# Two modulation products: row scaling on ScalarE and summing by accumulating DMAs, in place of fused multiply-adds on VectorE

## The chip, the cores and the metric

The kernel runs on one core of one Trainium2 chip. The metric is the time of one execution on the device in microseconds (us). Beside it stands one execution that the hardware profiler recorded, with every instruction of TensorE (PE, and PEld for its weight loads), VectorE (DVE), ScalarE (ACT), GpSimd (POOL) and SyncE (SP), and every DMA.

## The reference, cut to what matters

The program is a chain of four layers with 512 tokens of width 2048. The change touches only the modulation vectors of layers 3 and 4. They depend on one vector c and not on the tokens:

```python
def ada_modulation(c, w_mod, b_mod):
    m = jax.nn.silu(c) @ w_mod + b_mod
    shift, scale, gate = jnp.split(m, 3, axis=-1)
    return shift[:, None, :], scale[:, None, :], gate[:, None, :]
...
h = rms_norm(x, norm_g) * (1.0 + scale) + shift
out = mixer(h)
x = x + gate * out
```

There are two such products (`ab` and `sg`), each of a vector of 2048 with a matrix of 2048 x 6144.

## The kernel before

All large products run on PE as three matmuls each (`mm3`, L167: high by high, high by low, low by high), with weights that stream from HBM. SP loads a chunk of 128x1024 (`w_load`, L135), ACT rounds it to its high part (`w_high`, L150), DVE subtracts to get the low part (`w_low`, L156). The order of every engine's instructions is the order in which the program text issues them. SP has the weight loads and the loads of the modulation matrices; POOL has the loads and stores of the residual stream (L590, L483) and the small DMAs.

The main products call `pump()` (L86) after every 12 matmuls or so. A pump resumes each side task once (evictions, attention heads, gates) and then resumes the first background task `bg_rate` times. The two modulation products are that background task. `bg_rate` is 1 in layers 1 (from the second product on, for 32 pumps), 2 and 3; it is 2 in items j = 1 and j = 2 of the first out projection (`out_proj` with i = 0, L586, 16 pumps each), and 0 elsewhere in the out projections and in the rest of layer 1.

`modulation` (L1283) goes through the parts scale, shift, gate, and in each through four column blocks of 512. For one block it loads 16 tiles of 128x512 (256 KB each, L1293), two ahead of their use, and adds them up in `acc` on DVE: the first by `tensor_scalar` (L1299), the other 15 by `scalar_tensor_tensor` (L1301), with the column `sc[:, k]` of silu(c) as scalar. Each resume does one tile. Then it waits `bg_rate` resumes, splits `acc` into a high and a low part (`split`, L173: ACT rounds at L174, DVE subtracts at L175), waits again, lets PE add over the partitions with a matrix of ones (L1310, L1311), waits again, and copies the row of sums (L1315) to DRAM (L1316, from POOL). When a part is done, POOL loads it as columns (L1318) and DVE adds the bias (L1322).

The tiles `acc`, `raw`, `hi`, `lo` and `row` come from the pool `s` of 28 buffers, which nearly all side work uses too. PE executes its instructions in program order, those of the modulation among the matmuls of the item that is running.

Of the kernel before, what the change touches and what calls it, by code (L numbers as in the profile page):

```python
# [9 lines left out]
AF = mybir.ActivationFunctionType  # L10
ALU = mybir.AluOpType
# [4 lines left out]
D = 2048  # L16
KC = 16
# [3 lines left out]
LOOK = 1  # L21
# Between two layers, after each two k of: the last units' second token half, the next layer's first half, its second half.
# S sums of squares, P their 1/rms across partitions, c an operand chunk of this half, d one of the first half,
# h and l the two parts of a weight chunk. SCH_END: the same for the output.
SCH = [["", "", "S", "h", "Pl", "hc", "cl", "hc"],
       ["l", "h", "S", "", "Pl", "", "c", "c"],
       ["", "", "d", "hd", "dl", "d", "hd", "dl"]]
SCH_END = ["", "S", "", "P", "c", "c", "c", "c"]


class Core:
# [197 lines left out]
    def tm_item(self, evac, first=None, need=None, n=512):  # L229
        """first: the operand comes token half by token half, first.ensure(half, k) makes it."""  # L230
        ps = [self.ps() for _ in range(NT)]
        for half in range(2):
            if first and half == 0:
                cs = []
                for hf in range(2):
                    for c in range(4):
                        if hf == 0:
                            cs.append(self.w_get(1))
                        for kk in range(2):
                            k = 2 * c + kk  # L240
                            first.ensure(hf, k + LOOK)
                            for t in (2 * hf, 2 * hf + 1):
                                self.tm_mm(ps[t], t, *cs[c], kk, k, k == 0, False)
                            first.tick(1 + hf, k, c + kk if hf else 3 - c)
                            if kk:
                                self.pump()
                continue
            for c in range(4):
                if need and c == half == 0:
                    need(0)  # L250
                h, l = self.w_get(1 if need and half == 0 else LAG)
                for kk in range(2):
                    k = half * 8 + 2 * c + kk
                    if need:
                        need(k)
                    if first:
                        first.ensure(0, k + 2)
                        first.ensure(1, k + 2)
                    for t in range(NT):
                        self.tm_mm(ps[t], t, h, l, kk, k, k == 0, k == KC - 1, n)  # L260
                    if self.final_read:
                        self.final_read(k)
                    if k < KC - 1 and (kk or n == 512):
                        self.pump()
        self.add(evac(ps))
        self.pump()
# [21 lines left out]
    def fg_last(self, kperm, bd):  # L288
        """The last two units, token half by token half."""
        ps = [self.ps() for _ in range(2)]  # L290
        po = lambda hf, u: ps[hf][:, u * 256:(u + 1) * 256]
        cs = []
        for hf in range(2):
            sl = slice(256 * hf, 256 * hf + 256)
            for c in range(4):
                if hf == 0:
                    cs.append(self.w_get(4 - c))
                for kk in range(4):
                    i = 4 * c + kk
# [53 lines left out]

    # -- start: x from the input; 1/rms is applied to the first layer's products
    def start(self):
# [65 lines left out]

    # during a layer's last products: the mix that is done takes the place of operands that nothing reads any more
    def mix_early(self, kperm, mixk):
# [13 lines left out]

    # -- out projection of a layer, feature by feature: B gets x_new * gain, xd[i] the residual stream
    def out_proj(self, i, kperm, mixk, gain, gate=None, fg=None, shift=None, rx=None, final=False, dump=False):
# [187 lines left out]

    # ---------------- layer 1
    def plan1(self):
# [6 lines left out]
    def layer1(self):  # L636
        nc, a = self.nc, self.a
        P = dict(zip(("convw", "convb", "ba", "bx", "lam"), (0, 32, 40, 56, 72)))
# [22 lines left out]

        # log sigmoid of lambda, times 4, and half biases
        lsg = self.fix.tile([128, 32], F32, name="lsg")
# [309 lines left out]

    # ---------------- layer 2
    def plan2(self):
# [305 lines left out]

    # ---------------- modulation rows
    def modulation(self, w, i):  # L1283
        nc = self.nc
        for part in (1, 0, 2):
            for j in range(4):
                c0 = part * D + j * 512
                acc = self.s()
                raws = []
                for k in range(KC + 2):  # L1290
                    if k < KC:
                        raw = self.s()
                        nc.sync.dma_start(out=raw, in_=w[k * 128:(k + 1) * 128, c0:c0 + 512])  # L1293
                        raws.append(raw)
                    if k >= 2:
                        raw = raws.pop(0)
                        ck = self.sc[:, k - 2:k - 1]
                        if k == 2:
                            nc.vector.tensor_scalar(out=acc, in0=raw, scalar1=ck, scalar2=None, op0=ALU.mult)  # L1299
                        else:  # L1300
                            nc.vector.scalar_tensor_tensor(out=acc, in0=raw, scalar=ck, in1=acc, op0=ALU.mult, op1=ALU.add)  # L1301
                        yield
                for _ in range(self.bg_rate):
                    yield
                hi, lo = self.sr(), self.sr()
                self.split(hi, lo, acc)
                for _ in range(self.bg_rate):
                    yield
                ps = self.ps()
                nc.tensor.matmul(out=ps, lhsT=self.ones, rhs=hi, start=True, stop=False)  # L1310
                nc.tensor.matmul(out=ps, lhsT=self.ones, rhs=lo, start=False, stop=True)  # L1311
                for _ in range(self.bg_rate):
                    yield
                row = self.s()
                nc.scalar.copy(out=row[0:1], in_=ps[0:1])  # L1315
                nc.gpsimd.dma_start(out=self.md[i][part:part + 1, j * 512:(j + 1) * 512], in_=row[0:1])  # L1316
            dst = self.mcol[:, i, part]
# [21 lines left out]

    # ---------------- layer 3  # L1340
    def plan3(self):
# [148 lines left out]

    # ---------------- layer 4
    def plan4(self):
# [111 lines left out]

    # ---------------- whole
    def run(self):
# [41 lines left out]

# [1 line left out]

# [30 lines left out]
def layout(inp):  # L1681
    d = {}
# [3 lines left out]
    w = inp["even_w_in"][0]  # L1686
# [14 lines left out]
    c, s = np.cos(ang).astype(f), np.sin(ang).astype(f)  # L1701
# [15 lines left out]
    d["lruw"] = np.stack([wa[0], wa[1], wx[0], wx[1]], 2).reshape(8, 128, 512)  # L1717
    # layer 2
    w = inp["odd_w_in"][0]
# [12 lines left out]
    for nm in ("ab", "sg"):  # L1732
        d[nm + "_wm"] = inp[nm + "_w_mod_2"][0]
    # layer 3
    w = inp["ab_w_in_2"][0]
# [14 lines left out]
    d["bias3"] = np.where(cnt > 0, np.log(np.maximum(cnt, 1)) * 128.0 ** 0.5, -1e30).astype(f)  # L1750
    # layer 4
    w = inp["sg_w_in_2"][0]
# [30 lines left out]
```

## Time and profile before

| | before |
|---|---|
| median of 3 runs (us) | 3378.86 |
| lowest and highest (us) | 3377.93, 3380.07 |
| span of the profiled execution (us) | 3376.1 |
| busy, PE and PEld | 99%, 82% |
| busy, DVE | 56% |
| busy, ACT | 36% |
| busy, POOL | 3% |

The span counts from the first to the last instruction of the profiled execution. Busy time on PE is modelled and overlaps: a matmul of 512 columns stands as 0.39 us, and the next one starts about 0.23 us after it. So PE's pace is read from the starts, and its idle time from the waits. Instructions that only issue a DMA count as no busy time.

### The profile page before, as it was taken

To read this page: it belongs to the slowest core of one execution; us is meant where nothing else is said; L and a number is where in the kernel's file an instruction comes from. 1 tells how busy PE (TensorE), PEld (TensorE's weight loads), DVE (VectorE), ACT (ScalarE), POOL (GpSimd) and SP (SyncE) were. 2 spreads that over 40 slices of the span, in tenths; PEclk is the share of its full clock that TensorE was granted. 3 is DMA by queue.
4 is the path that set the end of the run, shared out by engine and by line. 5 is a ranking of instruction groups with operands and counts; after the bars stand their busy time and mean duration, and the time that the engine had idled before them with its cause. 6 is when DMAs were issued, how large, how long until landed. Compare 5 with 4: busy or idle time off the path is not lost.

```text
span 3376.1 us, 40334 instructions
## 1 busy us (share of the span) xinstructions
PE 3354.3 (99%) x15596; PEld 2766.4 (82%) x15596; DVE 1894.8 (56%) x3179; ACT 1223.4 (36%) x1966; POOL 113.5 (3%) x208
## 2 busy tenths in 40 slices
PE   9999999999999999999999999999999999999998
PEld 7888888888888888888888888888888888888887
DVE  7766676568656566564576665544434526533334
ACT  5355553343333233344542322322333424222332
POOL 0000000100000000001000000000000000000000
PEclk9999999999999999999999999999999999999999
DMA  5422235645454445444344444322333422223232
GB/s 207 153 81 81 76 103 182 202 133 173 153 162 152 157 153 179 136 156 145 123 141 156 149 161 171 109 88 88 112 125 129 144 96 88 97 97 107 95 107 92
DMA packets 155088, 443.92 MB, mean 131 GB/s; under 512 B 19429, under 2 KB 19557, under 8 KB 154896
## 3 DMA queue, kind: packets, MB, share of 16 engines
q1 hardware_dynamic: 140832, 398.95, 35.5%
q0 software_dynamic: 14064, 42.40, 4.0%
q8 instruction: 122, 2.00, 0.2%
q14 instruction: 70, 0.57, 0.1%
HBM read 424.36 MB, written 16.91 MB: 131 GB/s over the span
## 4 chain that ended last, share of the span: by engine, by line
PE 99%; DVE 0%; DMA 0%; ACT 0%; issue 0%; SPq 0%; DVEq 0%; ACTq 0%
PE ps L169 32%; PE ps L171 32%; PE ps L170 32%; PE ps L178 2%; DMA raw<-in_w1t 0%; PE ps L1310 0%; PE ps L1311 0%; PE ps L519 0%; DVE s L529 0%; PE ps L505 0%; DVE l L156 0%; SPq L366 0%; ACT h L150 0%; ACT B L484 0%; ACT s L479 0%
## 5 line engine op out<-in xcount | busy, mean ns | idle before, releaser
L169 PE MATMUL ps<-Ah,h 128*128 128x512 f32 (+1 forms) x3200 | 1240.2, 388 | 0.0
L171 PE MATMUL ps<-Ah,l 128*128 128x512 f32 (+1 forms) x3200 | 1230.1, 384 | 0.0
L170 PE MATMUL ps<-Al,h 128*128 128x512 f32 (+1 forms) x3200 | 1225.2, 383 | 0.0
L156 DVE TENSOR_TENSOR l<-raw,h 128x1024 fp32r<-128x1024 f32 (+2 forms) x559 | 675.0, 1209 | 735.4 <-ACT h L150 726.5
L150 ACT CAST h<-raw 128x1024 fp32r<-128x1024 f32 (+2 forms) x559 | 577.3, 1035 | 863.2 <-PE ps L170 503.0
L171 PEld LDWEIGHTS ps<-Ah,l 128*128 128x128 f32 x3200 | 601.7, 188 | 127.9
L170 PEld LDWEIGHTS ps<-Al,h 128*128 128x128 f32 x3200 | 602.1, 188 | 122.8 <-issue 0.2
L169 PEld LDWEIGHTS ps<-Ah,h 128*128 128x128 f32 x3200 | 602.3, 188 | 117.4 <-issue 0.2
L169 PE MATMUL ps<-h,Ah 128*128 128x512 f32 (+2 forms) x1408 | 547.9, 389 | 7.1 <-ACT h L174 5.8
L170 PE MATMUL ps<-l,Ah 128*128 128x512 f32 (+2 forms) x1408 | 543.9, 386 | 0.8 <-DVE l L156 0.8
L171 PE MATMUL ps<-h,Al 128*128 128x512 f32 (+2 forms) x1408 | 544.2, 386 | 0.4
L169 PEld LDWEIGHTS ps<-h,Ah 128*128 128x128 f32 x1408 | 265.5, 189 | 64.1 <-ACT h L174 5.8
L171 PEld LDWEIGHTS ps<-h,Al 128*128 128x128 f32 x1408 | 265.2, 188 | 60.9 <-DVE Al L551 1.6
L170 PEld LDWEIGHTS ps<-l,Ah 128*128 128x128 f32 x1408 | 265.4, 189 | 57.9 <-DVE l L156 1.1
L1301 DVE SCALAR_TENSOR_TENSOR s<-s,sc 128x512 f32<-128x512 f32 x360 | 268.8, 747 | 5.8 <-DMA s<-in_ab_wm 1.7
L175 DVE TENSOR_TENSOR s<-ps,s 128x512 fp32r<-128x512 f32 (+2 forms) x178 | 101.1, 569 | 153.8 <-ACT s L174 153.7
L174 ACT CAST s<-ps 128x512 fp32r<-128x512 f32 (+2 forms) x178 | 86.1, 491 | 242.9 <-PE ps L178 168.1
L169 PE MATMUL ps<-s 128*128 128x512 f32 (+2 forms) x384 | 131.6, 343 | 0.0
L171 PE MATMUL ps<-s 128*128 128x512 f32 (+2 forms) x384 | 129.5, 337 | 1.3 <-DVE s L175 1.3
L170 PE MATMUL ps<-s 128*128 128x512 f32 (+2 forms) x384 | 128.8, 335 | 0.0
L476 ACT ACTIVATE s<-s 128x512 f32<-128x512 f32 (+1 forms) x72 | 42.0, 583 | 136.3 <-DVE s L468 73.3
L171 PEld LDWEIGHTS ps<-s 128*128 128x128 f32 x384 | 72.5, 189 | 10.2 <-DVE s L175 1.5
(271 smaller groups left out, 2026.6 us busy)
## 6 DMA issues: line engine op xcount, KB each, us to landing
raw<-in_wo SPq DMA_DIRECT2D x128, 512.0 KB, 3.5
raw<-in_w3f SPq DMA_DIRECT2D x112, 512.0 KB, 3.5
s<-in_ab_wm SPq DMA_DIRECT2D x192, 256.0 KB, 4.2
s<-in_sg_wm SPq DMA_DIRECT2D x192, 256.0 KB, 4.1
raw<-in_w2t SPq DMA_DIRECT2D x88, 512.0 KB, 3.6
raw<-in_w4f SPq DMA_DIRECT2D x64, 512.0 KB, 3.5
raw<-in_w1f SPq DMA_DIRECT2D x48, 512.0 KB, 3.6
raw<-in_w2f SPq DMA_DIRECT2D x32, 512.0 KB, 3.6
```

What stands on the lines that cost most here:

```text
L150: self.nc.scalar.copy(out=h[:, 0:n], in_=raw[:, 0:n])
L156: self.nc.vector.tensor_tensor(out=l[:, 0:n], in0=raw[:, 0:n], in1=h[:, 0:n].bitcast(F32), op=ALU.subtract)
L169: mm(out=out, lhsT=lh, rhs=rh, start=start, stop=False)
L170: mm(out=out, lhsT=lh, rhs=rl, start=False, stop=False)
L171: mm(out=out, lhsT=ll, rhs=rh, start=False, stop=stop)
L174: self.nc.scalar.copy(out=h, in_=src)
L175: self.nc.vector.tensor_tensor(out=l, in0=src, in1=h.bitcast(F32), op=ALU.subtract)
L178: self.nc.tensor.transpose(out, src, self.idt)
L476: nc.scalar.activation(out=sq[0], in_=xn, func=AF.Square)
L1301: nc.vector.scalar_tensor_tensor(out=acc, in0=raw, scalar=ck, in1=acc, op0=ALU.mult, op1=ALU.add)
```

## The change

`modulation` now takes two column blocks at a time, each with its own `acc`, and goes through their 32 tiles in turn. The first tile of a block is loaded into `acc` itself. Each tile is loaded three resumes ahead, and ACT scales it in place (`activation`, Copy, `scale=sc[:, k]`). From the second tile of a block on, the scaled tile is put on a list, and one resume later POOL issues a DMA that adds it to `acc` (`accum_op=add`, SBUF to SBUF). No DVE instruction is left in this loop. After the last tile the remaining sum is issued, three resumes are waited, and then the two blocks are split, summed over the partitions and stored one after the other as before. The other lines of the diff drop comments.

```diff
         for part in (1, 0, 2):
-            for j in range(4):
...
-                    if k >= 2:
+            for jj in range(2):
+                acc = [self.s() for _ in range(2)]
+                col = lambda j: slice(part * D + (2 * jj + j) * 512, part * D + (2 * jj + j + 1) * 512)
+                raws, sums = [], []
+                for n in range(2 * KC + 3):
+                    if n < 2 * KC:
+                        k, j = divmod(n, 2)
+                        raw = acc[j] if k == 0 else self.s()
+                        nc.sync.dma_start(out=raw, in_=w[k * 128:(k + 1) * 128, col(j)])
                         raws.append(raw)
+                    if n >= 3:
+                        k, j = divmod(n - 3, 2)
                         raw = raws.pop(0)
-                        ck = self.sc[:, k - 2:k - 1]
-                        if k == 2:
-                            nc.vector.tensor_scalar(out=acc, in0=raw, scalar1=ck, scalar2=None, op0=ALU.mult)
-                        else:
-                            nc.vector.scalar_tensor_tensor(out=acc, in0=raw, scalar=ck, in1=acc, op0=ALU.mult, op1=ALU.add)
+                        nc.scalar.activation(out=raw, in_=raw, func=AF.Copy, scale=self.sc[:, k:k + 1])
+                        if k:
+                            sums.append((acc[j], raw))
+                    raw = None
+                    if len(sums) > (1 if n < 2 * KC + 2 else 0):
+                        x, y = sums.pop(0)
+                        nc.gpsimd.dma_start(out=x, in_=y, accum_op=ALU.add)
+                        x = y = None
+                    if n >= 3:
                         yield
+                while sums:
+                    x, y = sums.pop(0)
+                    nc.gpsimd.dma_start(out=x, in_=y, accum_op=ALU.add)
+                    x = y = None
+                for _ in range(3):
+                    yield
+                for j in range(2):
+                    hi, lo = self.sr(), self.sr()
+                    self.split(hi, lo, acc[j])
...
```

## Rows read from the trace of the kernel before

**Rows 1.** The page's head and part 1: busy us, share, instructions
```profile
span 3376.1 us, 40334 instructions
...
PE 3354.3 (99%) x15596; PEld 2766.4 (82%) x15596; DVE 1894.8 (56%) x3179; ACT 1223.4 (36%) x1966; POOL 113.5 (3%) x208
```

**Rows 2.** Waits of PE, us 690 to 1660: us in total, times, longest
```profile
PE ps L171 <- DVE s L175: 1.3, 1, 1.3
PE ps L178 <- DVE s L1170: 0.4, 1, 0.4
```

**Rows 3.** Busy time by stretch: us, engines busy (instructions), granted clock, DMA share, GB/s
```profile
0.00:14.00 14.00, 7.62 (x21) 5.19 (x22) 3.87 (x9) 5.41 (x8) 4.08 (x11) 1.00 0.80 269
...
18.00:22.00 4.00, 4.00 (x14) 3.15 (x13) 4.00 (x9) 3.39 (x6) 0.00 (x0) 0.66 1.03 394
...
544.00:633.00 89.00, 89.00 (x390) 73.00 (x389) 54.80 (x72) 29.35 (x38) 11.36 (x20) 1.00 0.75 255
...
820.00:832.00 12.00, 10.30 (x74) 9.34 (x73) 10.38 (x29) 5.29 (x13) 2.33 (x4) 1.00 0.68 210
...
1680.00:2146.00 466.00, 465.89 (x2053) 379.81 (x2054) 303.96 (x492) 146.35 (x231) 4.66 (x8) 1.00 0.46 154
...
3360.00:3377.00 17.00, 4.23 (x27) 3.25 (x25) 7.70 (x18) 1.72 (x5) 0.00 (x0) 0.67 0.50 190
```

**Rows 4.** Lines L1301, L1299: count, ns minimum/median/maximum, first and last start
```profile
L1301 DVE SCALAR_TENSOR_TENSOR s<-s,sc x360: 644/747/754, 61.8 to 2145.9; 128x512 f32<-128x512 f32 x180
...
L1299 DVE TENSOR_SCALAR s<-s,sc x24: 477/481/489, 59.4 to 2091.6; 128x512 f32<-128x512 f32 x24
```

**Rows 5.** ACT by line and shape: busy us, mean ns, idle before and releaser
```profile
L174 ACT CAST s<-s 128x512 fp32r<-128x512 f32 x58 | 35.0, 618 | 117.0 <-DVE s L1379 101.3 <-DVE s L1301 14.2 <-DVE s L834 1.5
...
L479 ACT ACTIVATE s<-s,cols 128x512 f32<-128x512 f32 x14 | 9.9, 709 | 0.0
```

**Rows 6.** Timeline of PE, first out projection: start, us, instruction (13th after the first)
```profile
566.22 0.39 PE L169 MATMUL ps<-Ah,h 128*128 128x512 f32 x1
...
568.97 0.39 PE L169 MATMUL ps<-Ah,h 128*128 128x512 f32 x1
```

**Rows 7.** Timeline of DVE, us 543 to 566
```profile
543.90 1.53 DVE L1301 SCALAR_TENSOR_TENSOR s<-s,sc 128x512 f32<-128x512 f32 x2
...
551.92 0.69 DVE L175 TENSOR_TENSOR s<-s 128x512 fp32r<-128x512 f32 x1 [0.43 <-ACT s L174]
...
557.12 1.54 DVE L1301 SCALAR_TENSOR_TENSOR s<-s,sc 128x512 f32<-128x512 f32 x2
...
559.71 1.53 DVE L1301 SCALAR_TENSOR_TENSOR s<-s,sc 128x512 f32<-128x512 f32 x2
```

**Rows 8.** Timeline of POOL: the loads at the start of item j = 2
```profile
588.90 1.13 POOL L590 DMA_DIRECT2D s<-in_x  x2
```

**Rows 9.** DMA issues, us 544 to 633: count, KB each, median us to landing
```profile
s<-in_ab_wm SPq DMA_DIRECT2D x41, 256.0 KB, 6.0
...
xd<-s POOLq DMA_DIRECT2D x8, 256.0 KB, 6.2
...
md<-s POOLq DMA_DIRECT2D x3, 2.0 KB, 4.9
```

**Rows 10.** Line L483 (POOL's stores from SBUF), us 1480 to 1660
```profile
L483 POOL DMA_DIRECT2D xd<-s x14: 540/542/545, 1539.0 to 1656.2; - x14
...
DMA to landing us min/median/max: 2.3/2.3/2.6
```

**Rows 11.** Waits of POOL, us 544 to 640
```profile
POOL mcol L1318 <- DMA md<-s: 4.7, 1, 4.7
```

**Rows 12.** DMA issues, us 832 to 1152: a POOL load in layer 2
```profile
s<-rd POOLq DMA_DIRECT2D x6, 256.0 KB, 6.0
```

**Rows 13.** Timeline of all engines, us 815 to 842
```profile
823.39 0.49 DVE L1299 TENSOR_SCALAR s<-s,sc 128x512 f32<-128x512 f32 x1 [1.18 <-DMA s<-in_ab_wm]
...
828.71 0.19 PEld L171 LDWEIGHTS ps<-s 128*128 128x128 f32 x1 [1.50 <-DVE s L175]
```

More of the change, by code (lines that the diff above doesn't have):

```diff
@@ L1285, in modulation @@
         for part in (1, 0, 2):
-            for j in range(4):
[L1287 to L1293, printed above, removed]
+            for jj in range(2):
[7 more added lines that the diff above has]
+                        nc.sync.dma_start(out=raw, in_=w[k * 128:(k + 1) * 128, col(j)])
@@ L1303, in modulation @@
-                for _ in range(self.bg_rate):
-                    yield
[L1305 to L1313, printed above, removed]
@@ L1314, in modulation @@
-                row = self.s()
-                nc.scalar.copy(out=row[0:1], in_=ps[0:1])
-                nc.gpsimd.dma_start(out=self.md[i][part:part + 1, j * 512:(j + 1) * 512], in_=row[0:1])
+                        nc.scalar.activation(out=raw, in_=raw, func=AF.Copy, scale=self.sc[:, k:k + 1])
[6 more added lines that the diff above has]
+                        x = y = None
@@ new lines, in modulation @@
+                    if n >= 3:
+                        yield
+                while sums:
[3 more added lines that the diff above has]
+                for _ in range(3):
+                    yield
+                for j in range(2):
+                    hi, lo = self.sr(), self.sr()
+                    self.split(hi, lo, acc[j])
+                    for _ in range(self.bg_rate):
+                        yield
+                    ps = self.ps()
+                    nc.tensor.matmul(out=ps, lhsT=self.ones, rhs=hi, start=True, stop=False)
+                    nc.tensor.matmul(out=ps, lhsT=self.ones, rhs=lo, start=False, stop=True)
+                    for _ in range(self.bg_rate):
+                        yield
+                    row = self.s()
+                    nc.scalar.copy(out=row[0:1], in_=ps[0:1])
+                    nc.gpsimd.dma_start(out=self.md[i][part:part + 1, (2 * jj + j) * 512:(2 * jj + j + 1) * 512], in_=row[0:1])
```

## The prediction

> **What bounds the kernel now.** I read the page's busy times first, then PE's waits, then the table by stretch, then the pace of PE in its timeline. PE is busy for 3354.3 of 3376.1 us [rows 1]; DVE, which the change relieves, for 56%. Of the 21.8 us in which PE is idle, most lie where no modulation runs: 6.4 us in the first 14 us and some 12 us after us 3360, up to the span's end [rows 3]. In between, PE waits for DVE twice, for 1.3 and 0.4 us [rows 2], both around 826 us in layer 2. So a free DVE can give back 1.7 us at the most. The pace of PE between waits is 12 matmuls in 568.97 - 566.22 = 2.75 us [rows 6]. The change adds and removes no matmul. What is left to ask is whether it makes PE wait.
>
> **The change part by part.** *Removed from DVE:* 360 x 0.747 + 24 x 0.481 = 280 us [rows 4]. It lies beside PE's work and gives the path at most the 1.7 us above.
>
> *Added to ACT:* 384 scalings. The nearest row is L479, the same Copy with a column as scale from SBUF to SBUF, at 0.709 us [rows 5]: 272 us, which takes ACT from 1223 to 1495 us, 44% of the span. In the fullest stage, us 544 to 633, 38 scalings add 27 us to 29 busy of 89 [rows 3]. PE hides that; without that cover it would be the 272 us.
>
> *A scaling waits for its tile's load.* DVE had this wait before. Queued behind it on ACT are now the weight roundings (L150) and the roundings that feed PE. The load is issued three resumes ahead instead of two, so in the steady state I cost it at nothing. In layer 2 at 823 us, where pumps follow each other without an item's matmuls, DVE waited 1.18 us for such a load and PE 1.50 us for DVE a little later [rows 13]. There the new order has the first scaling of a pair of blocks two pumps later (step 34 of layer 2, counted as below). The bounds are -1.7 us (PE's waits for DVE go) and +6.0 us (a whole landing [rows 9]); I take 0, since one wait replaces another of its kind.
>
> *Added to POOL:* 360 DMA issues at 0.54 us each, as a store of the same tile costs [rows 10], 194 us on an engine that is busy for 113. But POOL takes its instructions in order, and each accumulation must wait until the previous one on the same `acc` has landed; POOL's load of `md` shows such a wait on one of its own DMAs, 4.7 us [rows 11]. With two sums in turn, each `acc` gets one accumulation per two resumes, and a block is a chain of 15 landings. The Trainium skill (DMA: Bandwidth & Descriptors, Rules for kernel authors) states the same: two accumulations on the same bytes need a wait for the first one's semaphore. Without that order there would be no chain, and the sum would be 0.
>
> *At rate 1* a round of the chain has two pumps, 5.5 us at the pace of rows 6 and more with attention in between: in layer 3 some 110 tiles took 466 us, 8.5 us per round. A load on POOL's queue in layer 2 lands in 6.0 us [rows 12]. That fits, and the last accumulation has four pumps before the split. I cost it at nothing.
>
> *At rate 2*, in items j = 1 and 2 of the first out projection, both resumes fall in one pump: DVE's pairs at 557.12 and 559.71 us show it [rows 7]. Between the first pair (543.90 [rows 7]) and the loads of item j = 2 (588.90 [rows 8]) lie 16 pumps, so a pump is 2.8 us and a round must land in 2.8 us. I count the 64 resumes of this stage in the new code. The 32 of layer 1 have just done the first pair's tiles. Its end takes 3 + 2 x 4 = 11. The second pair takes steps 12 to 43 for the tiles; its first accumulation goes out at step 15 (pump 8, 543.9 + 7 x 2.8 = 563.5 us); the first split is at step 47, and the first matmul with ones at step 49, in pump 25. PE ended item j = 0 just before 543.3 us, so it gets there at 543.3 + 25 x 2.8 = 613.3 us. That matmul stands in PE's own order, so no prefetched weights help it: it waits for the 15th landing, ACT's rounding (0.62 us [rows 5]) and DVE's subtraction (0.69 us [rows 7]). With L for issue to landing, the stall is 563.5 + 15 L + 1.3 - 613.3 = 15 L - 48.5 us, which is zero up to L = 3.2 us.
>
> *What is L?* No accumulating DMA is in the trace. From below: POOL's store of the same 256 KB where the queues are quiet, 2.3 us [rows 10], which reads only once. From above: the same store in this very stage, 6.2 us; there the modulation loads take 6.0 and even a 2 KB store 4.9 [rows 9]. The DMA engines are 75% busy here at 255 GB/s [rows 3], which is 340 GB/s when busy, so 256 KB in one pass cost 0.77 us. The 34 accumulations of the stage add 26 us (one pass) or 52 us (two reads of SBUF) to 67 of 89 us: 104% to 134%. So the engines stay full while loads go on, and I take L = 6.1 us until PE stalls: 8 rounds, to 612.3 us. Once PE stands, the weight loads stop, and L falls to the quiet store plus a second pass, 2.3 + 0.77 = 3.07: 7 rounds take 21.5 us. The chain ends at 633.8, and the stall is 633.8 + 1.3 - 613.3 = 21.8 us. The bounds are 0 (L below 3.2) and 15 x 6.1 - 48.5 = 43 us.
>
> The Trainium skill (DMA: Bandwidth & Descriptors, Anatomy of one DMA) gives a fixed 2.0 us plus the bytes at 436 GB/s for a DMA of POOL, 2.6 us for 256 KB as an estimate. By that rule the chain would keep up and the sum would be 0; the quiet store agrees with it and the store in this stage does not.
>
> *A stall's price on the clock.* After its idle time at the start PE has a mean granted clock of 0.66 from 18 to 22 us [rows 3], a mix of 2.4 and 1.2 GHz, which loses 0.34 x 4 = 1.4 us. I add that once, with 0 and 2 x 1.4 as bounds.
>
> *The buffers.* Tiles that wait for the chain stay in the pool of 28. At pump 21 about 14 rounds are due and 7 done, so some 14 tiles more are held, and SP may stand at a modulation load with weight loads behind it. That starves PE by another door, but ends when the same chain ends; I add nothing.
>
> Sum against the profiled execution: 3376.1 + 21.8 + 1.4 = 3399.3 us; the median of the runs lies 2.8 us above that span, so 3402 us.
>
> **The rivals.** *The chain keeps up (not slower).* Place: the same 15 landings; it decides at L = 3.2 us. For it: the quiet store at 2.3 us, and an accumulation does not touch HBM, which the slow 2 KB store does. Against it: loads and stores of both queues are slow in this stage. Then only the 1.7 us of PE's waits can go: 3377 to 3379 us.
>
> *Later stages stall too.* If accumulations need more than the 8.5 us of a round in layers 2 and 3, each of the other ten pairs ends late: at 9.5 us by 15 us each, 150 us less the four pumps of spare time each, about 40 us more, 3440 us. For it: the DMA share there is 0.46 [rows 3] and would rise to 0.6 or 0.8. Against it: the slowest rows are near 6 us.
>
> *DVE was the hidden bound (faster).* 280 us leave DVE, but PE waited for it for 1.7 us: 3377 us. A gain of over 0.2% has no row behind it.
>
> **How the numbers follow.** Stall in the first out projection: 0.66, 3385 to 3424 us. Chain keeps up: 0.22. Later stages too: 0.08. Something no row shows: 0.04. I predict 3402 us. The range goes from 3377 (kept up, PE's two waits gone) to 3427 us (L = 6.1 throughout, 43 us, with the clock, and a few us of layer 2's wait). About 0.2%, 6.8 us, is what a measurement of this kernel can tell from no change. A stall of under 6.8 us takes 0.03 of the first case, so: slower 0.71, same 0.25, faster 0.04.
>
> **What would show it.** Right: PE's waits have one entry of about 20 us at the matmul with ones (the old L1310), near 613 us; POOL shows waits on its own accumulations in us 565 to 635 and few elsewhere; the DMA share there is near 1; the accumulations land in about 6 us there and under 5 us in layer 3; the granted clock dips once after the stall. DVE falls to about 1615 us and ACT rises to about 1495. Wrong: landings below 3.2 us in that stage with no wait of PE there, or waits of PE on ACT spread over layers 2 and 3, which would mean that ACT's order, and not POOL's chain, is what costs.

## The result, and the profile after

| | before | after |
|---|---|---|
| median (us), runs of the comparison | 3378.39 | 3439.52 |
| lowest and highest (us) | 3377.38, 3380.07 | 3435.70, 3442.38 |
| ratio, 95% interval | | 1.0182 [1.0168, 1.0197] |
| span of the profiled execution (us) | 3376.1 | 3437.6 |

The change costs 61 us. The prediction had the sign and the place of one wait (its size too, but partly by chance), and a range (3377 to 3427 us) that ends 12.5 us short of the result.

In the code after, the modulation's load stands at L1294, the scaling on ACT at L1299, the accumulating DMA at L1305 and L1311, the matmuls with ones at L1321 and L1322. The other lines named here keep their numbers. First the head and part 1 of the page after, against [rows 1]:

```profile
span 3437.6 us, 41168 instructions
...
PE 3367.4 (98%) x15596; PEld 2772.6 (81%) x15596; DVE 1649.9 (48%) x2795; ACT 1458.4 (42%) x2350; POOL 420.6 (12%) x568
```

PE has the same 15596 matmuls. The work went where it was meant to go: 245 us off DVE, 235 us onto ACT, and 307 us onto POOL. POOL's 307 us are the issues of the accumulating DMAs, which the trace does count as busy time on this engine, unlike what is said of them above. What makes PE wait is in the waits of PE over the whole span (us in total, times, longest), of which [rows 2] shows the part in layer 2:

```profile
PE ps L1321 <- ACT s L174: 21.0, 1, 21.0
PE ps L169 <- ACT h L150: 13.1, 1, 13.1
PE ps L178 <- DVE s L1170: 8.4, 4, 4.1
...
PE ps L178 <- DVE s L1171: 4.6, 1, 4.6
```

Left out are one of 8.1 us at the start (5.8 us in the kernel before) and some of 1.7 us or less. The table by stretch says where these are; its columns are those of [rows 3], and the first and last rows have their like there:

```profile
544.00:633.00 89.00, 71.18 (x300) 57.05 (x298) 22.98 (x26) 40.95 (x59) 24.79 (x33) 0.91 0.92 250
633.00:700.00 67.00, 50.70 (x233) 42.12 (x234) 20.92 (x26) 22.84 (x32) 17.57 (x25) 0.84 0.74 205
820.00:900.00 80.00, 74.22 (x405) 63.20 (x404) 49.31 (x118) 40.80 (x79) 20.20 (x27) 0.96 0.81 216
900.00:1680.00 780.00, 771.96 (x3566) 633.96 (x3566) 341.29 (x688) 365.50 (x628) 151.34 (x195) 1.00 0.73 198
1680.00:2146.00 466.00, 465.33 (x2150) 382.98 (x2150) 236.72 (x384) 223.78 (x351) 89.46 (x112) 1.00 0.75 201
```

PE is idle for 34.1 us in the first out projection (17.8 and 16.3 us in the two stretches) and runs there at a lower clock; it is idle for 13.8 us in layer 2 (5.8 and 8.0; 1.7 and 0.2 in the kernel before), and hardly in layer 3. The DMA share of layer 3 rose from 0.46 [rows 3] to 0.75.

Each of the two large groups, in the trace after: the second wait ends with a rounding on ACT that waited for the last landing of the chain; and in layer 2 an engine after the other waits for DMAs into tiles of the shared pool before PE does. These are ACT's, DVE's and PE's rows of the timeline (start, us, instruction, idle before and its releaser):

```profile
648.63 0.62 ACT L174 CAST s<-s 128x512 fp32r<-128x512 f32 x1 [19.09 <-DMA s<-s]
...
888.97 0.40 ACT L1159 ACTIVATE s<-s,misc 128x128 f32<-128x128 f32 x1 [3.98 <-DMA s<-s]
890.36 0.29 DVE L1162 SCALAR_TENSOR_TENSOR s<-ps,s 128x128 f32<-128x128 f32 x1 [7.42 <-DMA s<-s]
892.83 0.69 DVE L1164 SCALAR_TENSOR_TENSOR s<-ps,s 128x512 f32<-128x512 f32 x1 [2.17 <-DMA s<-s]
...
894.89 1.23 PE L178 MATMUL ps<-idt,s 128*128 128x128 f32 x4 [4.58 <-DVE s L1171]
```

L1157 to L1164 are the attention heads of layer 2. They read nothing that the modulation makes, and the operands of L1162 come from PE and ACT. The only tie between them and an accumulation is the pool: what they wait for is the tile that they write, which an accumulation that has not landed still reads. (The trace does not name the single buffer; that the waits go with more buffers is shown below, e11.) The first stall of the out projection has the same kind of row ahead of it, at L476, the square in the eviction:

```profile
599.62 0.63 ACT L476 ACTIVATE s<-s 128x512 f32<-128x512 f32 x1 [6.28 <-DMA s<-s]
...
611.80 0.63 ACT L476 ACTIVATE s<-s 128x512 f32<-128x512 f32 x1 [8.77 <-DMA s<-s]
...
622.96 0.80 PE L169 MATMUL ps<-Ah,h 128*128 128x512 f32 x1 [13.10 <-ACT h L150]
```

The weight rounding L150 stands behind L476 on ACT, and PE behind L150. The kernel before has no DMA from a tile to a tile, and so no such wait.

### The profile page after: what moved, and what is told of

The parts are those of the page before. It is cut to its first block, busy times and chain, and to the rows that moved or that the text cites. A ratio compares the mean times of both kernels' runs of the same rounds, so it can differ in the third digit from the quotient of the medians.

```text
span 3437.6 us, 41168 instructions
## 1 busy us (share of the span) xinstructions
PE 3367.4 (98%) x15596; PEld 2772.6 (81%) x15596; DVE 1649.9 (48%) x2795; ACT 1458.4 (42%) x2350; POOL 420.6 (12%) x568
## 3 DMA queue, kind: packets, MB, share of 16 engines
q0 software_dynamic: 65904, 136.79, 19.7%
## 5 line engine op out<-in xcount | busy, mean ns | idle before, releaser
L169 PE MATMUL ps<-Ah,h 128*128 128x512 f32 (+1 forms) x3200 | 1241.5, 388 | 13.1 <-ACT h L150 13.1
L171 PE MATMUL ps<-Ah,l 128*128 128x512 f32 (+1 forms) x3200 | 1232.2, 385 | 0.0
L150 ACT CAST h<-raw 128x1024 fp32r<-128x1024 f32 (+2 forms) x559 | 576.3, 1033 | 714.4 <-PE ps L170 454.3
L169 PEld LDWEIGHTS ps<-Ah,h 128*128 128x128 f32 x3200 | 603.5, 189 | 131.4 <-ACT h L150 13.5
L171 PEld LDWEIGHTS ps<-Ah,l 128*128 128x128 f32 x3200 | 602.6, 188 | 128.4 <-DVE l L156 0.8
L169 PE MATMUL ps<-h,Ah 128*128 128x512 f32 (+2 forms) x1408 | 548.5, 390 | 8.1 <-ACT h L174 8.1
L171 PE MATMUL ps<-h,Al 128*128 128x512 f32 (+2 forms) x1408 | 544.4, 387 | 0.3 <-DVE Al L551 0.2
L1305 POOL DMA_DIRECT2D s<-s x348 | 297.0, 862 | 1031.4 <-ACT s L1299 369.5
L169 PEld LDWEIGHTS ps<-h,Ah 128*128 128x128 f32 x1408 | 266.1, 189 | 64.5 <-ACT h L174 8.1
L171 PEld LDWEIGHTS ps<-h,Al 128*128 128x128 f32 x1408 | 265.8, 189 | 60.5 <-DVE Al L551 1.6
L1299 ACT ACTIVATE s<-s,sc 128x512 f32<-128x512 f32 x384 | 266.8, 718 | 43.1 <-DMA s<-in_ab_wm 35.5
L169 PE MATMUL ps<-s 128*128 128x512 f32 (+2 forms) x384 | 132.6, 345 | 1.4 <-ACT s L174 1.3
L171 PE MATMUL ps<-s 128*128 128x512 f32 (+2 forms) x384 | 130.3, 339 | 0.6 <-DVE s L175 0.6
L590 POOL DMA_DIRECT2D s<-xd x48 | 26.0, 593 | 779.2 <-PE ps L171 301.4
```

The costliest lines, as they stand in the source:

```text
L150: self.nc.scalar.copy(out=h[:, 0:n], in_=raw[:, 0:n])
L169: mm(out=out, lhsT=lh, rhs=rh, start=start, stop=False)
L171: mm(out=out, lhsT=ll, rhs=rh, start=False, stop=stop)
L590: nc.gpsimd.dma_start(out=x, in_=xsrc[4 * j + u])
L1299: nc.scalar.activation(out=raw, in_=raw, func=AF.Copy, scale=self.sc[:, k:k + 1])
L1305: nc.gpsimd.dma_start(out=x, in_=y, accum_op=ALU.add)
```

## The experiments

Four theories were put against each other. C: the chain of landings at the doubled rate, as predicted. B: buffers, tiles held by accumulations that have not landed. S: ScalarE's additional work and its scaling in order. D: the accumulating DMAs as a whole (C and B together). All ratios are against the kernel before on the same chip.

| run | us | ratio, interval |
|---|---|---|
| e1: adds on DVE | 3378.57 | 1.0001 [0.9991, 1.0011] |
| e2: scaling on DVE | 3437.93 | 1.0177 [1.0162, 1.0192] |
| e3: 29 tiles | 3447.07 | 1.0204 [1.0189, 1.0219] |
| e4: 29 tiles, rate 1 | 3440.56 | 1.0185 [1.0170, 1.0201] |
| e5: before, private pool | 3397.19 | 1.0057 [1.0042, 1.0072] |
| e6: after, private pool | 3482.83 | 1.0313 [1.0296, 1.0330] |
| e7: after, private pool, rate 1 | 3459.38 | 1.0238 [1.0222, 1.0253] |
| e8: pairs | 3389.38 | 1.0031 [1.0018, 1.0044] |
| e9: before, no low parts | 3375.54 | 0.9994 [0.9985, 1.0004] |
| e10: after, no low parts, 28 tiles | 3441.82 | 1.0186 [1.0171, 1.0202] |
| e11: the same, 36 tiles | 3418.00 | 1.0122 [1.0105, 1.0139] |
| e12: the same, 36 tiles, rate 1 | 3392.80 | 1.0041 [1.0026, 1.0056] |
| e13: as e11, plain copies | 3397.65 | 1.0059 [1.0044, 1.0074] |
| e14: as e11, ones three pumps later | 3417.75 | 1.0119 [1.0104, 1.0134] |
| e15: as e12, pairs | 3376.08 | 0.9994 [0.9985, 1.0004] |

### Which part of the change costs: e1 and e2

e1 keeps the scaling on ACT and the loads, and adds on DVE:

```diff
-                        nc.gpsimd.dma_start(out=x, in_=y, accum_op=ALU.add)
+                        nc.vector.tensor_tensor(out=x, in0=x, in1=y, op=ALU.add)
```

> Everything of the change stays (ScalarE scales, two sums in turn, the same loads in the same order) but the adds: VectorE adds the scaled tiles, no accumulating DMA. Theory D (the 61 us come from the accumulating DMAs: their landings, their chains, the tiles that they hold): 3375 to 3390 us, and the waits of TensorE at the matmul with ones and of ScalarE for tiles that DMAs hold are gone. Theory S (the rival: ScalarE pays, by 267 us more of work and by scaling in order behind late loads): 3425 to 3440 us, nothing gained.

e2 keeps the DMAs and scales on DVE:

```diff
-                        nc.scalar.activation(out=raw, in_=raw, func=AF.Copy, scale=self.sc[:, k:k + 1])
+                        nc.vector.tensor_scalar(out=raw, in0=raw, scalar1=self.sc[:, k:k + 1], scalar2=None, op0=ALU.mult)
```

> The accumulating DMAs stay, VectorE does the 384 scalings in place of ScalarE. Theory D: 3425 to 3445 us, with the wait of some 21 us at the matmul with ones as before. Theory S: 3378 to 3395 us. If the loads' lateness is what counts, whoever scales, it stays above 3425 too, but the waits of TensorE move from ScalarE's results to VectorE's.

Measured: 3378.57 and 3437.93 us. With all of ACT's new work and no accumulation the kernel stands where it stood before; with all accumulations and none of ACT's new work it stands where the change put it. S falls, D stays. The page of e1 (part 1) shows the work on ACT that costs nothing:

```profile
PE 3353.7 (99%) x15596; PEld 2769.4 (82%) x15596; DVE 1860.6 (55%) x3155; ACT 1457.5 (43%) x2350; POOL 113.4 (3%) x208
```

In e2 the stalls stay in their places (24.1 us at the matmul with ones, 11.6 us at L169), although ACT is down to 1224 us.

### One tile more, and the single rate: e3 and e4

```diff
-        self.p_s = pool(name="s", bufs=28)
-        self.p_t = pool(name="tiny", bufs=24)
+        self.p_s = pool(name="s", bufs=29)
+        self.p_t = pool(name="tiny", bufs=19)
...
-            self.bg_rate = 2 if i == 0 and j in (1, 2) else 0
+            self.bg_rate = 1 if i == 0 and j in (1, 2) else 0
```

e3 has the first two lines, e4 all.

> The changed kernel with 29 tiles in the shared pool in place of 28 (room from five of the small 32-column tiles). Theory B (buffers: other engines' tiles wait for a tile that a landing accumulation still reads, about 13 us in the first out projection and about 20 us in layer 2): 5 to 25 us faster, 3415 to 3435 us. Theory C (the chain of landings at the doubled rate makes all of it): 3439 us, unchanged within 3, and the 21 us wait at the matmul with ones stays in both.

> As the one with 29 tiles, but the first out projection asks for one step of the product at each pump, not two. Theory C: some 35 to 40 us faster than that one: no wait of TensorE over 5 us from 544 to 700 us. Theory B alone: the wait at the matmul with ones goes all the same, but the rest does not: 10 to 20 us slower than before stay, spread over layer 2 (3388 to 3400 us). If the load of the DMA engines as such is the cause: less than 10 us faster.

Measured: 3447.07 and 3440.56 us. Theories B and C expected neither time; the time of e4 alone would fit the load of the DMA engines as such, since it is only 6.5 us faster than e3. One tile more made it 7.6 us slower. So B, as far as e3 was to show it, was missed; why one tile more costs and not gains is left open (which tile is reused next changes all over the program). e4 is the more telling one. Its table by stretch:

```profile
544.00:633.00 89.00, 89.00 (x391) 73.08 (x390) 31.16 (x34) 43.49 (x61) 23.34 (x33) 1.00 0.90 266
633.00:700.00 67.00, 67.00 (x389) 58.60 (x388) 40.56 (x90) 29.95 (x56) 11.81 (x20) 1.00 0.52 151
820.00:900.00 80.00, 52.89 (x226) 42.31 (x227) 36.26 (x113) 34.28 (x72) 16.97 (x21) 0.80 0.72 172
```

In the first out projection both stalls are gone, at a DMA share of 0.90: C is right there, and load of the DMA engines as such is not what costs there. But the steps that were not done there are done at the start of layer 2, and PE loses 27.1 us from 820 to 900 (5.8 in the kernel after). Waits of DVE and ACT in e4, us 800 to 900:

```profile
DVE s L1162 <- DMA s<-s: 20.7, 3, 8.3
DVE s L175 <- DMA s<-s: 8.6, 1, 8.6
...
ACT s L1159 <- DMA s<-s: 10.1, 3, 6.2
ACT s L1158 <- DMA s<-s: 8.9, 2, 6.3
ACT s L174 <- DMA s<-s: 8.4, 1, 8.4
```

These are waits for tiles, as B has them.

### Private tiles, too few of them: e5, e6 and e7

```diff
-        self.p_raw = pool(name="raw", bufs=3)
+        self.p_raw = pool(name="raw", bufs=2)
-        self.p_s = pool(name="s", bufs=28)
-        self.p_t = pool(name="tiny", bufs=24)
+        self.p_s = pool(name="s", bufs=25)
+        self.p_m = pool(name="m", bufs=6)
+        self.p_t = pool(name="tiny", bufs=19)
...
-                acc = [self.s() for _ in range(2)]
+                acc = [self.m() for _ in range(2)]
...
-                        raw = acc[j] if k == 0 else self.s()
+                        raw = acc[j] if k == 0 else self.m()
```

> The kernel before (adds on VectorE) with the tiles of the product (accumulators and loaded tiles) in a pool of six of their own; room for it from the shared pool (25 for 28), from the raw weight tiles (2 for 3) and five of the small tiles. It is the control for the next two: 3375 to 3390 us if the smaller pools cost little by themselves. More would be the price of the pools, to be taken off the next two.

> The changed kernel with the same private pool of six: no other engine's tile can then wait for an accumulation. Theory B: the waits of ScalarE and VectorE on DMAs for tiles in layer 2 go and TensorE's waits there with them (some 20 us), and the first stall in the first out projection (13 us) too; the wait at the matmul with ones stays, 15 to 30 us: 3400 to 3415 us, if the control costs nothing. If layer 2's loss is DMA load or ScalarE's order: 3435 us or more, with those waits in place.

> The private pool and one step at each pump in the first out projection together. Theories B and C together: both losses gone, 3378 to 3390 us (control's price on top). If anything else takes part, over 3395 us, with its wait to be read.

Measured: the control costs 18.3 us, and on top of it e6 costs 85.6 and e7 62.2 us. The three expectations were missed, those of e6 and e7 by far. The waits of ACT and SP in e6 say why (line numbers are 4 higher here):

```profile
ACT m L1303 <- DMA m<-in_ab_wm: 243.8, 109, 6.9
ACT m L1303 <- DMA m<-in_sg_wm: 199.1, 92, 5.6
...
SPq L1298 <- DMA m<-m: 870.6, 308, 10.0
```

No other engine's tile waits for an accumulation any more. But with six tiles, two of them accumulators, nearly every load (308 of 384) waits for a landing, so it comes late, and ACT stands at the scaling for 443 us where it stood for 43. The wait left by one door and came in by another. This doesn't refute B, since the same landings still hold too few tiles, and it doesn't show it either. What was wanted was more tiles.

### More tiles: e9 to e12

Room comes from the low parts of the weights (L166 to L168 here are L169 to L171 elsewhere, all other lines are 3 lower too):

```diff
-        self.p_l = pool(name="wl", bufs=4)
...
-            self.whl[self.wprep] = (h, l)
+            self.whl[self.wprep] = (h, h)
...
-        self.p_s = pool(name="s", bufs=28)
+        self.p_s = pool(name="s", bufs=36)
```

e9 (on the kernel before) and e10 have all but the last change; e11 has it; e12 has the single rate of e4 as well.

> The kernel before without the low parts of the weights: VectorE still subtracts, into the raw tile itself, and the product that takes the low part reads the high part again, so TensorE's work is the same and 16 KB of the SBUF come free (the pool wl). Pool of 28 as it was. Control: 3375 to 3381 us, the kernel before.

> The changed kernel without the low parts of the weights in the same way, pool of 28 as it was. Control: 3434 to 3444 us, with the waits of the changed kernel.

> As the control of the changed kernel (no low parts of the weights), the room given to the shared pool: 36 tiles for 28. Everything else, the landings, the chain, the doubled rate, ScalarE's scaling in order, is the same. Theory B (tiles held by landings make the engines wait): the waits of ScalarE and VectorE on DMAs for tiles go, layer 2 loses under 5 us, the stall of 13 us goes, the wait at the matmul with ones stays (15 to 25 us and some 3 us of clock): 3398 to 3412 us. If the loss in layer 2 has another cause (ScalarE's order, DMA load): over 3425 us.

> The same with 36 tiles and one step at each pump in the first out projection. Theories B and C together: nothing is left, 3376 to 3388 us. If it stays over 3400 us, a third cause is at work, which the waits of TensorE name.

Measured: 3375.54, 3441.82, 3418.00 and 3392.80 us. The controls are where they should be. Eight tiles more give back 23.8 us; the single rate on top of them gives back another 25.2 us, and 17.3 us remain over e9. That is 4.8 us more than the most that e12 was to have, and e11 is 6 us over its upper end. Two rows of the table by stretch, us 820 to 900 and 900 to 1680, first e10, then e11:

```profile
820.00:900.00 80.00, 72.88 (x414) 62.36 (x414) 49.67 (x112) 39.04 (x75) 19.69 (x26) 0.98 0.80 212
900.00:1680.00 780.00, 773.45 (x3569) 635.07 (x3568) 342.50 (x694) 366.54 (x633) 151.75 (x195) 0.99 0.74 199
```

```profile
820.00:900.00 80.00, 78.44 (x442) 67.36 (x440) 53.83 (x131) 44.04 (x88) 20.43 (x27) 1.00 0.85 229
900.00:1680.00 780.00, 780.00 (x3613) 641.70 (x3612) 347.89 (x689) 372.89 (x638) 152.72 (x197) 1.00 0.73 199
```

With 36 tiles PE stands nowhere from 900 to 1680 us, at the same DMA share and with nearly the same landings (median 5.3 us, 5.8 in e10): that is B. The waits of ACT and DVE for landings of accumulations did not go, as was expected, but fell to a fifth (from some 107 to some 23 us, us 800 to 1680). And PE's one long wait in e11, with POOL's accumulations ahead of it:

```profile
561.14 1.81 POOL L1302 DMA_DIRECT2D s<-s  x2 [2.32 <-ACT s L1296]
...
608.17 0.85 POOL L1302 DMA_DIRECT2D s<-s  x1 [2.35 <-DMA s<-s]
...
629.35 0.85 POOL L1302 DMA_DIRECT2D s<-s  x1 [5.06 <-DMA s<-s]
...
637.09 0.84 POOL L1302 DMA_DIRECT2D s<-s  x1 [0.88 <-DMA s<-s]
...
641.01 0.84 POOL L1302 DMA_DIRECT2D s<-s  x1 [1.45 <-DMA s<-s]
...
648.17 0.62 ACT L171 CAST s<-s 128x512 fp32r<-128x512 f32 x1 [34.85 <-DMA s<-s]
...
648.85 0.80 PE L1318 MATMUL ps<-s,ones 128*128 128x512 f32 x1 [36.47 <-ACT s L171]
```

Two rows of its chain that ended last (start, us, what), and the landings of the accumulations issued from 630 to 647 us:

```profile
640.52 0.49 issue
...
644.82 3.27 DMA s<-s
```

```profile
DMA to landing us min/median/max: 3.3/3.3/3.6
```

The 13 us stall ahead of it is gone, and the wait at the matmul with ones has grown to 36.5 us: in the kernel after, the two (13.1 + 21.0 = 34.1) were one late chain, paid in two places. The chain takes 648.17 - 561.14 = 87.0 us for 15 rounds, 5.80 us each. A round is a landing and some 0.5 us from it to the next issue (the 0.49 us above, in which POOL waits for nothing that the trace shows). The seven rounds up to 608.17 take 6.7 us each, the next three 7.1 us on average (their landings 8.2, 3.3 and 7.5 us), the quiet ones at the end 641.01 - 637.09 = 3.9 us.

### The price of a round, and the rest: e13, e14 and e15

e13 takes `accum_op=ALU.add` out of both DMAs of e11. e14 and e15 are:

```diff
-                for _ in range(3):
+                for _ in range(9 if self.bg_rate == 2 and jj == 1 else 3):
...
-                        if k:
+                        if k == 1:
                             sums.append((acc[j], raw))
+                        elif k > 1 and k % 2:
+                            nc.vector.tensor_tensor(out=raw, in0=raw, in1=half[j], op=ALU.add)
+                            sums.append((acc[j], raw))
+                            half[j] = None
+                        elif k:
+                            half[j] = raw
```

The first is e14; the second is e15 (on e12) and, on the kernel after with its 28 tiles and its doubled rate, e8.

> The kernel with 36 tiles and the doubled rate (no low parts of the weights), with plain copies in place of the accumulating DMAs: same tiles, same queue, same order, each copy waiting for the one before it on its accumulator; the sums are left out. If a landing is dear because an accumulation moves its bytes twice, a round falls from 5.8 to some 4 us and the wait at the matmul with ones from 36.5 to 15 x 4 - 48.5 = 11.5 us: some 3393 us. If a landing is dear because of the loads beside it, it stays 25 to 37 us: 3407 to 3418 us. If the order of the chain played no part: no change at all.

> The same kernel with 36 tiles and the doubled rate, with the accumulating DMAs; the matmul with ones of the second pair of sums comes six steps, three pumps, later in TensorE's order. Theory C (a chain of fixed length against TensorE's own progress): the wait falls by 3 x 2.8 = 8.4 us, from 36.5 to 28 us: 3409 us, within 3. If the wait were the price of DMAs as such, wherever TensorE stands: 3418 us.

> The changed kernel, 28 tiles and doubled rate as it was, but VectorE adds two scaled tiles and one accumulating DMA adds the pair: 8 accumulations in a sum for 15 (192 in all for 360). Theories B and C: a chain of 8 landings of 6.1 us is 49 us, what the block's last load leaves, so the wait at the matmul with ones is under 5 us; half as many tiles are held, so layer 2 loses 5 to 12 us: 3385 to 3400 us. Were the cost in proportion to the accumulations alone: 3378 + 61 x 192/360 = 3411 us.

> 36 tiles, one step at each pump, and pairs of scaled tiles added by VectorE so that 8 accumulations make a sum, not 15. The 15 us that 36 tiles and the single rate left over lie at the start of layer 2 (815 to 885 us), where engines still wait for tiles that accumulations hold. If that is theory B once more, they go: 3375 to 3383 us. If it is the modulation's other work there (scaling in order, loads), 3388 to 3393 us.

Measured: 3397.65, 3417.75, 3389.38 and 3376.08 us. PE's wait at the matmul with ones in e13, e14 and e8, in this order (L1327 is that matmul in e8):

```profile
PE ps L1318 <- ACT s L171: 19.0, 1, 19.0
```

```profile
PE ps L1318 <- ACT s L171: 28.7, 1, 28.7
```

```profile
PE ps L1327 <- ACT s L174: 7.0, 1, 7.0
```

e14: the wait fell by 7.8 us for three pumps of 2.8 us, as C says of a chain that runs against PE's own progress. The time did not fall; some of what was gained there was lost again at the start of layer 2, to which steps moved, as in e4 (us 820 to 900: PE 75.98 of 80 us at a clock of 0.98, 78.44 at 1.00 in e11). That is 2.5 us of idle time and some 1.6 us of clock; where the rest went is left open, and the four runs of each spread over 7 us. The expectation of the time was a miss: the number is that of the other branch, though the wait itself moved as C has it. e13: a plain copy makes the round shorter, and the wait is half. So what an accumulation costs over a copy is part of the price, and not all of it; whether by the length of its own landing or by what the chain adds to the load is not separated (the DMA share from 544 to 633 us falls from 0.92 to 0.80 too). e8: half the accumulations leave 10.5 us of 61, within the expected 3385 to 3400 us; the two parts were both off: 7.0 us of wait at the matmul with ones, where under 5 us were expected, and 2.1 us of idle time in layer 2, where 5 to 12 us were. e15: nothing is left (3376.08 us, e9 3375.54). In e12, from 815 to 885 us, DVE waits 9.8 us (L172) and ACT 7.9 us (L1154) for landings of accumulations; in e15 no engine waits for one there. That fits B, as its expectation had it; half the accumulations also bring half of their load, so e15 alone does not tell B from load.

No version here beats the kernel before by anything clear of the noise: e1 and e15 pay nothing and gain nothing. The waits of PE for DVE beside the modulation were 1.7 us [rows 2].

## Why the prediction was wrong

*The relief of DVE* was put at 1.7 us at the most. e15 agrees: its DVE is busy for 1753 us, that of its control e9 for 1894, and the times are the same. (e1 says little of this, since its DVE adds in place of multiplying: 1861 us.)

*ACT's work* was put at 272 us, hidden, and its wait for loads at nothing. Right: 384 scalings at 718 ns each, hidden (e1), and the same time whichever engine does them (e2). These are the rows of L1299 and of L1305 in the trace after (count, ns minimum/median/maximum, first and last start):

```profile
L1299 ACT ACTIVATE s<-s,sc x384: 703/718/743, 55.3 to 2227.3; 128x512 f32<-128x512 f32 x192
```

```profile
L1305 POOL DMA_DIRECT2D s<-s x348: 832/847/1291, 61.4 to 2228.3; - x174
```

*POOL's issues* were put at 0.54 us, from a store [rows 10]; an accumulation takes 0.85. The difference lies inside the round of the chain, 15 x 0.31 = 4.6 us of it.

*The chain at rate 2.* The mechanism was right: the stall goes with the single rate (e4, e12), follows PE's place by three pumps (e14), and with 36 tiles, where nothing else takes a share, a round of 5.80 us in the place of L gives 15 x 5.80 - 48.5 = 38.5 us against 36.5 measured. The term that was mis-sized is L, taken as 6.1 us for 8 rounds and 3.07 for 7, a mean of 4.7: 1.1 us a round too short, some 17 us. Half of it is a term that the formula left out: L was the time from issue to landing, and a round also has the 0.5 us from the landing to the next issue, some 8 us in 15 rounds. With it taken off, the first seven rounds landed in 6.2 us each, as predicted. The other half is above all the step "once PE stands, L falls": PE stood from 612 us, but of the three accumulations issued from 608 to 622 us two landed in 8.2 and 7.5 us, beside other transfers that did not stop at once: weights, and POOL's own loads and stores of the residual stream. The DMA issues of e11 from 608 to 630 us (count, KB, median us to landing):

```profile
s<-s POOLq DMA_DIRECT2D x7, 256.0 KB, 6.8
raw<-in_wo SPq DMA_DIRECT2D x3, 512.0 KB, 4.8
s<-in_x POOLq DMA_DIRECT2D x4, 256.0 KB, 5.8
xd<-s POOLq DMA_DIRECT2D x2, 256.0 KB, 7.1
```

And a quiet landing is 3.3 us, not 3.07. The 21.8 us of the prediction stand beside 21.0 us at the matmul with ones, but that agreement is partly chance: the chain's price was 34.1 us, of which 13.1 had been paid at L169. The upper bound of the prediction, 43 us, holds all of it. The fixed time and rate that the prediction cited from the Trainium skill (DMA: Bandwidth & Descriptors, Anatomy of one DMA), 2.6 us by estimate, were met by no accumulation: the shortest of 360 landed in 3.2 us.

*The clock* was put at 1.4 us. From 649 to 656 us, after the second stall, the trace after shows a granted clock of 0.58 (1.00 in the kernel before), between its two levels of 1.2 and 2.4 GHz: 0.42 x 7 = 2.9 us. From 623 to 628, after the first, it is 0.55: another 0.45 x 5 = 2.3 us. Two stalls, two prices, 5.2 us in all, where the prediction's bound was 2.8.

*The buffers* are the step that failed: "that starves PE by another door, but ends when the same chain ends; I add nothing". For the out projection it holds (the 13.1 us are the chain's own). But it looked for held tiles only where the chain is late. In layer 2 PE never waits at the matmul with ones, and still each scaled tile is held for the 5.7 us of its landing (median) and the wait for its turn, in a pool from which the attention heads take their tiles too. *At rate 1* the landing "fits" the round, and so the cost was put at nothing; the round was not what it had to fit. The price of this is most of the 23.8 us between e10 and e11: 12.1 us are PE's idle time in the four rows above (5.6 and 6.5), and the clock makes some 6 more, since it is down in e10 after three of the waits (0.51 from 897 to 903 us, 0.57 from 1319 to 1323, 0.58 from 1449 to 1453) and at 1.00 in e11 in the same three stretches. The rest lies outside layer 2.

In the kernel after, the chain then has 34.1 us of PE's idle time and 5.2 us of clock: 39 us, where 21.8 + 1.4 = 23.2 us were forecast, but inside the prediction's bounds. Layer 2 has 13.8 - 1.9 = 11.9 us of idle time more than before and some 6 us of clock (0.53 from 895 to 901 us, 0.57 from 1317 to 1321, 0.66 from 1446 to 1451): 18 us, where nothing was forecast and the one bound, 6 us, was for a late load. That put the result outside the range. Together 57 of the 61 us.

The sum by experiments: e10 to e11, 23.8 us, tiles; e11 to e12, 25.2 us, the doubled rate; e12 to e15, 16.7 us, which fits tiles again, held by the steps that the single rate moves to the start of layer 2. Together 65.7 us, all that separates e10 from e15. The split between the two depends on the order in which they are taken away: at 29 tiles the single rate gives 6.5 us only (e3, e4).

*The rivals.* "Later stages stall too" gave 3440 us, and the result is 3439.5; yet its mechanism is not what happened. It wanted landings over 8.5 us and late chains in layers 2 and 3; the landings in layer 3 are 5.9 us (median of 92), and PE waits at a matmul with ones once only, in the first out projection. "The chain keeps up" and "DVE was the hidden bound" fell with the 34 us.

*What was to show it.* The DMA share of 0.92, landings of about 6 us in the first out projection (median 5.4) and the PE wait near the place came. Landings under 5 us in layer 3 (5.9) and a single dip of the clock did not. Nor did the sign of being wrong come as it was written: PE's waits in layer 2 are on DVE, and e2 shows that ACT's scaling is not what costs. "POOL shows waits on its own accumulations in us 565 to 635 and few elsewhere" did not come either: this is POOL's row after for the whole span, of which 25.8 us lie in that stretch.

```profile
POOL s L1305 <- DMA s<-s: 331.2, 134, 6.6
```

## What to carry to other kernels

When work moves from an engine to DMAs, count how long each tile is held, not only how busy the engines are: a tile that was free 0.75 us after its multiply started is now free only when its accumulation has landed (5.7 us here), and in a shared pool whoever writes that tile next pays, in an engine's order that has nothing to do with the change. A chain of DMAs into one accumulator is as long as its count times a round, which is the loaded landing and the time to the next issue (0.5 us here); here the rounds got quick only some 17 us after the bound engine had stopped; and the matmul that needs the sum must stand that far behind. And if the engine that is relieved ended no wait of the bound engine, there is nothing to set against such a price.

## What the runs showed of the hardware

An SBUF to SBUF accumulation of 256 KB costs more of packets, DMA engine time, issue time and landing time than a plain copy of the same bytes. From the DMA queues of the kernel after and of e13 (packets, MB, share of the 16 engines):

```profile
q0 software_dynamic: 65904, 136.79, 19.7%
```

```profile
q0 software_dynamic: 42864, 136.79, 11.2%
```

The kernel before has 14064 packets and 4.0% on this queue. So an accumulation has (65904 - 14064) / 360 = 144 packets and takes (0.197 x 3437.6 - 0.040 x 3376.1) / 360 = 1.5 us of all 16 engines, a copy 80 packets and (0.112 x 3396.4 - 135) / 360 = 0.7 us. POOL's issue takes 0.85 against 0.54 us, a quiet landing 3.3 us (e11) against 2.3 us (e13, us 623 to 630), and a quiet round of the chain 3.9 against 2.8 us (626.21 - 623.43 in e13):

```profile
623.43 0.54 POOL L1302 DMA_DIRECT2D s<-s  x1 [0.85 <-DMA s<-s]
...
626.21 0.54 POOL L1302 DMA_DIRECT2D s<-s  x1 [1.36 <-DMA s<-s]
```
